# Dilated attention stage: the second head group's projections read the layer input in natural order, and the rewriting of that input between the first two groups goes

## The chip, the cores and the metric

One core of a Trainium2 chip. The metric is the device time of one execution in microseconds (us); lower is better. For the kernel before it is 3289.02 us, the median of 3 runs (3288.62 to 3292.9).

## What is computed

Two layers of an encoder on 1024 tokens of width 1024, all in float32. The change lies in the second layer's token mixer, a dilated sliding-window attention with three groups of 16 heads of width 64. Cut to what matters:

```
DIL_GROUPS = ((128, 1), (512, 4), (2048, 16))
def dilated_mixer(h, pos, w_in, g_q, g_k, rel_bias, w_o):
    proj = (h @ w_in).reshape(B, S, N_DIL_GROUPS, 3, DIL_HEADS, DIL_HEAD_DIM)
    for gi, (window, dilation) in enumerate(DIL_GROUPS):
        q = rms_norm(proj[:, :, gi, 0], g_q[gi])
        k = rms_norm(proj[:, :, gi, 1], g_k[gi])
        o, lse = dilated_group(q, k, proj[:, :, gi, 2], pos, table, window, dilation)
...
def _to_residues(t, dilation):
...
    t = t.reshape((B, L, dilation) + t.shape[2:])
    t = jnp.moveaxis(t, 2, 1)
```

Group 0 has dilation 1, group 1 dilation 4, group 2 dilation 16. Within a group a query sees only tokens whose number has the same remainder by the dilation, so the kernel works on tokens sorted by that remainder ("residue order"). The three outputs are merged by their softmax denominators.

## The kernel before, in words

The kernel runs on one core; a scheduler lays out the instructions of each engine, with the order of TensorE pinned to the program's in this stage. The dilated stage (`dil`) is a list of steps, `steps`: for each group, for each of 8 pairs of heads (`pr`), four steps (`tp`), each of which projects two tiles of 128 tokens. After the 32 steps of groups 0 and 1 stands one `None` step, after those of group 2 six. A `None` step projects nothing: it lets the attention work catch up, which lags the projections by some steps.

One step on TensorE consists of:

- `psav`: the products of the transposed probabilities `pT` with the values, of an earlier step,
- `pss`: 12 score products on `kT`, the stacked queries and keys of an earlier step,
- `psproj`: 24 matmuls for the first tile of 128 tokens,
- `psq`: four transposes of the step before's normalised q and k, `qn`,
- `psproj`: 24 matmuls for the second tile.

The 24 matmuls come from `project` (L1772): 8 chunks of the width, and for each three matmuls of `mm3` (L412 to L416), since each float32 operand is held as a high part and a low part. In them the **layer input is the stationary operand** (128 x 128, so a weight load of 128 tokens by 128 features goes ahead of each matmul), and the weights `wqkh`, `wqkl` are the moving operand of 256 columns.

The input lies transposed in SBUF, features on partitions and tokens along the free axis, in tiles of (128, 2, 512) float32: `hT`, `hTh`, `hTl`, `hsh` and `hsl`, in natural order of tokens. `permute` (L2077) rewrites it. Between groups 0 and 1 it writes 16 new tiles `hTp` in residue order of 4 with 32 copies of 128 x 512, which read every fourth token. Between groups 1 and 2 it writes 16 more `hTp` in residue order of 16 from the first 16, with 64 copies of 128 x 256. The copies go round ACT, DVE, ACT, DVE, POOL (L2092 to L2099). Two of the eight pairs of tiles are rewritten in the last step of a group, six in the `None` step.

From 1668 to 1952 us of the profiled execution group 0 is projected, from 1967 to 2247 us group 1, until 2544 us group 2.

The weights of a pair of heads (`wqkr`, four DMAs of 256 KB) are loaded two steps ahead (`fetch`, L2054, `dil_weights`, L1542 to L1551) by DMAs issued on ACT's queue; ACT and DVE then split them into `wqkh` and `wqkl`. The first pair's load is issued on SP's queue in the stage before. SP's queue also issues the loads of the bias tiles `bt`, the DMA transposes `pT<-ph` and the stores of `U`. All working tiles named here come from one pool of 29 buffers.

Of the kernel before, what the change touches and what calls it, by code (L numbers as in the profile page):

```python
# [9 lines left out]
F32 = mybir.dt.float32  # L10
# [4 lines left out]
AF = mybir.ActivationFunctionType  # L15
ALU = mybir.AluOpType
# [4 lines left out]
P = 128  # L21
# [20 lines left out]
class K:  # L42
# [1706 lines left out]
    def dil(self, at0, at1, tail, wqk, vd):  # L1749


        nc, a, tc = self.nc, self.a, self.tc
# [16 lines left out]
        ln14 = dpool.tile([P, 1], F32, name="ln14", bufs=1)  # L1769
        nc.vector.memset(ln14, 14.0 * math.log(2.0))  # L1770

        def project(h, w, ps, i, t):  # L1772
            tl = slice((t % 4) * P, (t % 4 + 1) * P)
            for d in range(ND):
                self.mm3(ps[:, i * 256 : (i + 1) * 256], h[t // 4](0, d)[:, tl], h[t // 4](1, d)[:, tl],
                         w[d // 4][0][:, d % 4, :], w[d // 4][1][:, d % 4, :], d == 0, d == ND - 1)

        def v_load(g, c):
# [59 lines left out]
        def stacks(u, tp, qn):  # L1838

            ps = PS("psq")  # L1840
            for k in range(2):
                for i in range(2):
                    c = i * 256 + (1 - k) * P
                    nc.tensor.transpose(ps[:, (2 * k + i) * P : (2 * k + i + 1) * P], qn[:, c : c + P], self.ident)
            s1 = 4 + tp % 2
            hi, lo = (u["k"][:, k, :].rearrange("p (s x) -> p s x", x=256)[:, tp : s1 + 1 : s1 - tp, :] for k in range(2))
            x = ps.rearrange("p (k x) -> p k x", k=2)
            nc.scalar.activation(hi, x, AF.Copy)
            nc.vector.tensor_tensor(lo, x, hi.bitcast(F32), op=ALU.subtract)
            for i in range(2):  # L1850
                c = S + (tp % 2 * 2 + i) * P
                u["q"][2 * tp + i] = u["k"][:, :, c : c + P]
# [181 lines left out]
        def um(u, hfs):  # L2034

            u.setdefault("um", [])
            v = Ud[u["pr"]].rearrange("(l t r) k e -> r l t (k e)", t=8, r=2)
            for hf in hfs:
                x = self.G("um", (P, 4, 2, P), F32)
                for i in range(2):  # L2040
                    nc.scalar.dma_start(out=x[64 * i : 64 * i + 64].rearrange("p t k e -> p t (k e)"), in_=v[i][:, 4 * hf : 4 * hf + 4, :])
                u["um"].append(x)
# [2 lines left out]

        steps = []
        for g in range(3):
            steps += [("qk", g, pr, tp) for pr in range(8) for tp in range(4)] + [None] * (1 if g < 2 else 6)
        loads, wts = {}, {}
        mark = len(nc.cur_bb.bb.instructions)  # L2050
        end = max(n for n, x in enumerate(steps) if x is not None)
        firsts = {n: s for n, s in enumerate(steps) if s is not None and s[3] == 0}

        def fetch(n):  # L2054
            if n in firsts:
                loads[n] = self.dil_weights(*firsts[n][1:3], eng=nc.scalar)

        def fetch_split(n):
            if n in firsts:
                wts[firsts[n][0:3]] = loads.pop(n)()  # L2060
# [9 lines left out]
                    vtodo.setdefault(n - 2 + t // 2, []).append(lambda t=t, VS=VS: v_parts(VS["raws"], VS, t))  # L2070
                vtodo.setdefault(n - 2 + t // 2, []).append(lambda VS=VS: VS.pop("raws"))

        h = [at0, at1]
        HT = [at0.tiles, at1.tiles]
        new = None

        def permute(g, dp, k):  # L2077

            for th in range(2):
                x = self.G("hTp", (P, 2, 512))  # L2080
                new[th][k].append(x)
                for oh in range(2):
                    src = HT[oh][k][dp].bitcast(F32)
                    if g == 1:
                        i_ = src.rearrange("p d (l r) -> p d r l", r=4)[:, :, 2 * th : 2 * th + 2, :]
                        copies = [(x.rearrange("p d (r b l) -> p d r b l", r=2, b=2)[:, :, :, oh, :], i_)]
                    else:
                        i_ = src.rearrange("p d (b l a) -> p d a b l", b=2, a=4)
                        o_ = x.rearrange("p d (a b l) -> p d a b l", a=2, b=4)
                        copies = [(o_[:, :, q, 2 * oh : 2 * oh + 2, :], i_[:, :, 2 * th + q]) for q in range(2)]  # L2090
                    for o_, i_ in copies:
                        e = permute.n % 5  # L2092
                        permute.n += 1
                        if e in (0, 2):
                            nc.scalar.activation(o_, i_, AF.Copy)
                        elif e in (1, 3):
                            nc.vector.tensor_copy(o_, i_)
                        else:
                            nc.gpsimd.tensor_scalar(o_, i_, 1.0, 1.0, op0=ALU.mult, op1=ALU.mult)  # L2099

        permute.n = 0
        perms = []
        units = {}
        transposed, scored, ready, carry, stacking, stk, late = [], [], [], [], None, [], []
        src = lambda pp, i, th: oTd[2 * pp : 2 * pp + 2, th, :, i, :].rearrange("r p f -> p r f")
        wts[("qk", 0, 0)] = wqk
        for n in sorted(vtodo):
            if n < 0:
                for f in vtodo.pop(n):
                    f()  # L2110
        for n, step in enumerate(steps):
            fetch(n + 2)
            for f in vtodo.pop(n, ()):
                f()
            if step is None and perms:
                while perms:
                    permute(*perms.pop(0))
                HT = new
                h = [(lambda k, d, t=t: t[k][d // 2][:, d % 2, :]) for t in HT]
            if step is not None and n + 1 < len(steps) and steps[n + 1] is None and step[1] < 2:  # L2120
                new = [[[], []], [[], []]]
                perms = [(step[1] + 1, dp, k) for dp in range(4) for k in range(2)]
                for _ in range(2):
                    permute(*perms.pop(0))
            w = None
            if step is not None:
                kind, g, pr, tp = step
                w = wts[(kind, g, pr)]
                if tp == 0:
                    units[(g, pr)] = {"g": g, "pr": pr, "q": {}, "V": VSs[(g, pr // 2)],  # L2130
                                      "k": D_("kT", (P, 2, S + 512), F32R, 2), "U": self.G("U", (P, 8, P), F32)}
                u = units[(g, pr)]
            fetch_split(n + 1)
            transposed, scored = scored, attend(ready, n > end) if ready else []
            for u_, t_, _ in scored:
                if u_["g"] == 2:
                    if u_["pr"] < 7:
                        if t_ == 7:
                            um(u_, (0, 1))
                    elif t_ in (1, 5):  # L2140
                        um(u_, (t_ // 4,))
            if step is not None:
                ps = PS("psproj")
                project(h, w, ps, 0, 2 * tp)
            ready, carry = carry, []
            stk.append(stacking)
            if len(stk) > 1:
                x = stk.pop(0)
                if x is not None:
                    stacks(*x)  # L2150
                    u_, tp_ = x[:2]
                    if u_["g"] == 2:
                        ready = ready + [(u_, 2 * tp_), (u_, 2 * tp_ + 1)]
                    else:
                        ready = ready + ([(u_, 2 * tp_ - 1), (u_, 2 * tp_)] if tp_ else [(u_, 0)])
                        carry = [(u_, 7)] if tp_ == 3 else []
            if step is not None:
                project(h, w, ps, 1, 2 * tp + 1)
                if step[1:3] == (2, 7):
                    tail(tp)  # L2160
            late, merged[:] = late + merged, []
            while late and (step is None or late[0][1] < n):
                u_, _, ths = late.pop(0)
                emit(u_, ths)
            for x in transposed:
                x[0]["at"] = n
                av(*x)
            stacking = None
            if step is not None:
                stacking = (u, tp, qkstep(u, tp, ps))  # L2170
                if n == end:
                    self.pin_from(mark, mybir.EngineType.PE)
                    banks.close()
                    first = banks.enter_context(tc.tile_pool(name="psY", bufs=4, space=PSUM, reuse_waits="tile"))
                    psp[0] = ctx.enter_context(tc.tile_pool(name="psT", bufs=4, space=PSUM, reuse_waits="tile"))
                    for pp in range(3):
                        self.reload(O, src, pp, 0, nc.sync)
# [171 lines left out]
```

## Time and profile before

| | |
|---|---|
| median of 3 runs | 3289.02 us |
| profiled execution, its own time | 3286.91 us |
| its span in the trace | 3285.1 us |
| mean granted TensorE clock | 0.983 |
| dilated stage's projections, first to last | 1668 to 2544 us |
| loads of `wqkr` issued on ACT's queue, on SP's queue | 92, 4 |

PE stands for TensorE's matmuls, PEld for its weight loads, DVE, ACT and POOL for VectorE, ScalarE and GpSimd, SP for the queue of SyncE. A matmul's recorded duration is longer than the distance between two starts, since they are pipelined: the rate is read from the starts. A row of groups names source line, engine, operation, output and inputs by tile names, shapes and count, then the total in us and the mean in ns, then the idle time of the engine ahead of it with what ended it.

### The profile page before, as it was taken

To read this page: it belongs to the slowest core of one execution; us is meant where nothing else is said; L and a number is where in the kernel's file an instruction comes from. 1 tells how busy PE (TensorE), PEld (TensorE's weight loads), DVE (VectorE), ACT (ScalarE), POOL (GpSimd) and SP (SyncE) were. 2 spreads that over 40 slices of the span, in tenths; PEclk is the share of its full clock that TensorE was granted. 3 is DMA by queue.
4 is the path that set the end of the run, shared out by engine and by line. 5 is a ranking of instruction groups with operands and counts; after the bars stand their busy time and mean duration, and the time that the engine had idled before them with its cause. 6 is when DMAs were issued, how large, how long until landed. Compare 5 with 4: busy or idle time off the path is not lost. (4 is left out here: it accounts for less than half of the span.)

```text
span 3285.1 us, 50852 instructions
## 1 busy us (share of the span) xinstructions
PE 3143.2 (96%) x18034; PEld 2653.5 (81%) x18034; DVE 2406.5 (73%) x4272; ACT 1736.5 (53%) x3507; POOL 878.6 (27%) x1197
## 2 busy tenths in 40 slices
PE   6989999999999999899999989998999899999999
PEld 6877677778888788778889889997988788888887
DVE  5677777757987866787657777777888678778566
ACT  5547787745544433542246676667565355444342
POOL 7455555520111000001133334434333001110010
PEclk8999999999999999999999989998999999999999
DMA  5352233152654788536557877777677635438554
GB/s 189 123 182 91 94 94 100 57 185 87 211 188 162 283 246 281 171 103 210 194 141 167 171 169 171 184 169 160 152 174 180 198 98 203 148 142 321 204 192 129
DMA packets 538990, 552.31 MB, mean 168 GB/s; under 512 B 199493, under 2 KB 421106, under 8 KB 538730
## 3 DMA queue, kind: packets, MB, share of 16 engines
q1 hardware_dynamic: 452362, 418.88, 44.9%
q0 software_dynamic: 27360, 91.31, 7.5%
q10 hardware_dynamic: 59008, 38.81, 4.6%
q8 instruction: 144, 2.36, 0.3%
q14 instruction: 116, 0.95, 0.1%
HBM read 376.17 MB, written 132.62 MB: 155 GB/s over the span
## 5 line engine op out<-in xcount | busy, mean ns | idle before, releaser
L415 PE MATMUL psm<-dl,dh 128*128 128x512 f32 x896 | 351.2, 392 | 8.1 <-DVE dl L122 8.0
L414 PE MATMUL psm<-hf,wf 128*128 128x512 f32 x896 | 350.1, 391 | 2.6 <-ACT wf L121 2.6
L416 PE MATMUL psm<-dh,dl 128*128 128x512 f32 x896 | 350.1, 391 | 0.0
L415 PE MATMUL psm<-hf,wf 128*128 128x512 f32 x896 | 349.2, 390 | 0.0
L416 PE MATMUL psm<-hf,wf 128*128 128x512 f32 x896 | 347.3, 390 | 0.4 <-DVE wf L122 0.4
L414 PE MATMUL psm<-dh,dh 128*128 128x512 f32 x896 | 334.8, 391 | 4.7 <-ACT dh L121 4.7
L414 PE MATMUL psproj<-wqkh,hTp 128*128 128x256 f32 x1024 | 303.2, 296 | 0.0
L415 PE MATMUL psproj<-wqkl,hTp 128*128 128x256 f32 x1024 | 291.1, 284 | 0.0
L416 PE MATMUL psproj<-wqkh,hTp 128*128 128x256 f32 x1024 | 290.9, 284 | 0.0
L121 ACT ACTIVATE dh<-ufr 128x1024 fp32r<-128x1024 f32 x112 | 118.3, 1057 | 174.9 <-PE psm L416 51.4
L415 PEld LDWEIGHTS psm<-dl,dh 128*128 128x128 f32 x896 | 169.0, 189 | 46.0 <-DVE dl L122 11.3
L414 PEld LDWEIGHTS psproj<-wqkh,hTp 128*128 128x128 f32 x1024 | 197.6, 193 | 9.0 <-issue 0.9
L414 PEld LDWEIGHTS psm<-dh,dh 128*128 128x128 f32 x896 | 168.2, 188 | 42.2 <-ACT dh L121 7.0
L414 PEld LDWEIGHTS psm<-hf,wf 128*128 128x128 f32 x896 | 168.6, 188 | 40.3 <-ACT wf L121 5.5
L415 PEld LDWEIGHTS psproj<-wqkl,hTp 128*128 128x128 f32 x1024 | 197.9, 193 | 0.0
L416 PEld LDWEIGHTS psm<-hf,wf 128*128 128x128 f32 x896 | 168.5, 188 | 36.2 <-DVE wf L122 1.1
L416 PEld LDWEIGHTS psm<-dh,dl 128*128 128x128 f32 x896 | 169.1, 189 | 35.1
L416 PEld LDWEIGHTS psproj<-wqkh,hTp 128*128 128x128 f32 x1024 | 197.4, 193 | 0.0
L415 PEld LDWEIGHTS psm<-hf,wf 128*128 128x128 f32 x896 | 168.6, 188 | 34.6
L122 DVE TENSOR_TENSOR dl<-ufr,dh 128x1024 fp32r<-128x1024 f32 x112 | 136.5, 1219 | 78.1 <-ACT dh L121 58.3
L745 DVE TENSOR_REDUCE mx<-pmx 128x1 f32<-128x512 f32 x256 | 165.0, 681 | 27.6 <-PE pmx L743 27.4
L122 POOL TENSOR_TENSOR pl<-p,ph 128x1024 fp32r<-128x1024 f32 x58 | 141.3, 2436 | 136.1 <-ACT ph L121 125.9
(399 smaller groups left out, 8920.9 us busy)
## 6 DMA issues: line engine op xcount, KB each, us to landing
ufr<-uf SPq DMA_DIRECT2D x112, 512.0 KB
adaw<-in_ada_w SPq DMA_DIRECT2D x96, 512.0 KB
w2r<-in_mlp_w SPq DMA_DIRECT2D x96, 512.0 KB
w1r<-in_mlp_w SPq DMA_DIRECT2D x64, 512.0 KB
bt<-bias SPq DMA_DIRECT2D x128, 256.0 KB
wqkr<-in_dil_w_in ACTq DMA_DIRECT2D x92, 256.0 KB
qkv<-st SPq DMA_DIRECT2D x32, 512.0 KB
hraw<-qkv SPq DMA_DIRECT2D x32, 512.0 KB
```

The lines of the kernel that those rows point to most:

```text
L121: nc.scalar.activation(hi, src, AF.Copy)
L122: (lo_eng or nc.vector).tensor_tensor(lo, src, hi.bitcast(F32), op=ALU.subtract)
L414: mm(out, lh, rh, start=first, stop=False)
L415: mm(out, lh, rl, start=False, stop=False)
L416: mm(out, ll, rh, start=False, stop=last)
L745: nc.vector.tensor_reduce(maxes[h][:, 2 * j + b : 2 * j + b + 1], ps, op=ALU.max, axis=AX.X)
```

## The change

`tokens` is new: for group 1 it gives `project` a slice of the natural-order tiles that takes every fourth token, 128 elements 16 bytes apart; for groups 0 and 2 it gives the contiguous slices as before. The `None` step after group 0 goes, and so does the first rewriting. The second rewriting reads the natural-order tiles, every sixteenth token, with 32 copies of 128 x 512 in place of 64 of 128 x 256. The weights of groups 0 and 1 are loaded on SP's queue; those of group 2 stay on ACT's.

```
-        def project(h, w, ps, i, t):
-            tl = slice((t % 4) * P, (t % 4 + 1) * P)
+        def tokens(g, t, k, d):
+            if g == 1:
+                return HT[t % 2][k][d // 2][:, d % 2, :].rearrange("p (l r) -> p r l", r=4)[:, t // 2, :]
+            return HT[t // 4][k][d // 2][:, d % 2, (t % 4) * P : (t % 4 + 1) * P]
+
+        def project(g, w, ps, i, t):
             for d in range(ND):
-                self.mm3(ps[:, i * 256 : (i + 1) * 256], h[t // 4](0, d)[:, tl], h[t // 4](1, d)[:, tl],
+                self.mm3(ps[:, i * 256 : (i + 1) * 256], tokens(g, t, 0, d), tokens(g, t, 1, d),
...
-            steps += [("qk", g, pr, tp) for pr in range(8) for tp in range(4)] + [None] * (1 if g < 2 else 6)
+            steps += [("qk", g, pr, tp) for pr in range(8) for tp in range(4)] + [None] * (0, 1, 6)[g]
...
-                loads[n] = self.dil_weights(*firsts[n][1:3], eng=nc.scalar)
+                loads[n] = self.dil_weights(*firsts[n][1:3], eng=nc.scalar if firsts[n][1] == 2 else nc.sync)
...
-                    src = HT[oh][k][dp].bitcast(F32)
-                    if g == 1:
-                        i_ = src.rearrange("p d (l r) -> p d r l", r=4)[:, :, 2 * th : 2 * th + 2, :]
-                        copies = [(x.rearrange("p d (r b l) -> p d r b l", r=2, b=2)[:, :, :, oh, :], i_)]
-                    else:
-                        i_ = src.rearrange("p d (b l a) -> p d a b l", b=2, a=4)
-                        o_ = x.rearrange("p d (a b l) -> p d a b l", a=2, b=4)
-                        copies = [(o_[:, :, q, 2 * oh : 2 * oh + 2, :], i_[:, :, 2 * th + q]) for q in range(2)]
+                    i_ = HT[oh][k][dp].bitcast(F32).rearrange("p d (l r) -> p d r l", r=16)[:, :, 8 * th : 8 * th + 8, :]
+                    o_ = x.rearrange("p d (r l) -> p d r l", l=64)[:, :, :, 32 * oh : 32 * oh + 32]
```

TensorE at the turn from group 0 to group 1, before: the last score products of group 0's last projected step, and then the `None` step's work, which has no `psproj`.

```order
L1869 MATMUL pss_25191<-kT_24580 128x256
L1869 MATMUL pss_25192<-kT_24580 128x256
L1844 MATMUL psq_25230<-ident,qn_24982 128x128 x4
L1937 LDWEIGHTS pT_25024
L1937 MATMUL psav_25237<-vs_24162,pT_25024 128x192
L1938 LDWEIGHTS pT_25024
```

The same place now: behind the score products stand the first projections of group 1, on `hT` tiles.

```order
L1873 MATMUL pss_25151<-kT_24592 128x256
L1873 MATMUL pss_25152<-kT_24592 128x256
L414 MATMUL psproj_25190<-wqkh_25003,hT_3811_18667 128x256
L415 MATMUL psproj_25190<-wqkl_25004,hT_3811_18667 128x256
L416 MATMUL psproj_25190<-wqkh_25003,hT_3812_18668 128x256
L414 MATMUL psproj_25190<-wqkh_25003,hT_3811_18667 128x256
```

No matmul is added or lost (26351 rows of TensorE in both); the `None` step's attention work moves into the first steps of group 1.

ACT at the same turn, before: between `ph`, the high part of the probabilities, and `wqkh`, the first weights of group 1, stand copies into `hTp`, and the square of the last projection (`dsq`) is in among them.

```order
L1923 ACTIVATE ph_25023<-pd_25039 128x512
L2095 ACTIVATE hTp_25150<-hT_3836_18782 128x4x128
L2095 ACTIVATE hTp_25153<-hT_3837_18783 128x4x128
L2095 ACTIVATE hTp_25156<-hTl_20785 128x4x128
L2095 ACTIVATE hTp_25159<-hsh_19483 128x4x128
L2095 ACTIVATE hTp_25165<-hT_3861_18892 128x4x128
L2095 ACTIVATE hTp_25168<-hT_3861_18892 128x4x128
L1828 ACTIVATE dsq_25126<-psproj_25050 128x512
L2095 ACTIVATE hTp_25171<-hsh_19487 128x4x128
L2095 ACTIVATE hTp_25174<-hsh_19487 128x4x128
L2095 ACTIVATE hTp_25180<-hT_3880_18987 128x4x128
L121 ACTIVATE wqkh_25183<-wqkr_24985 128x1024
```

Now nothing stands between `ph` and the first weights of group 1.

```order
L1927 ACTIVATE ph_24739<-pd_24754 128x512
L121 ACTIVATE wqkh_25003<-wqkr_24855 128x1024
L1832 ACTIVATE dsq_24840<-psproj_24764 128x512
L121 ACTIVATE wqkh_25007<-wqkr_24858 128x1024
L112 ACTIVATE drl_24845<-dms_24841,eps 128x8
```

All 13 copies on ACT are gone there, and the split of the weights follows the attention's rows at once.

SP's queue in group 0 now, at one pair's weight load: it stands behind a DMA transpose and a store of `U`, ahead of the next bias tiles and the next transpose.

```order
L1929 DMA_TRANSPOSE pT_22929<-ph_22928 128x16x128
L1959 DMA U<-U_21796 128x8x128
L1551 DMA wqkr_23181<-in_dil_w_in 128x4x128 x2
L1551 DMA wqkr_23184<-in_dil_w_in 128x4x128 x2
L1882 ISA
L1882 DMA bt_23220<-bias_135 128x2x256
L1882 ISA
L1882 DMA bt_23347<-bias_135 128x2x256
L1929 DMA_TRANSPOSE pT_23066<-ph_23065 128x16x128
```

Before, the four `wqkr` rows of this pair stood on ACT's queue, between `dsq` and the small steps of the normalisation, and here `bt` followed `U` directly.

More of the change, by code (lines that the diff above doesn't have):

```diff
@@ L2071, in dil, with permute @@
                 vtodo.setdefault(n - 2 + t // 2, []).append(lambda VS=VS: VS.pop("raws"))
-        h = [at0, at1]
         HT = [at0.tiles, at1.tiles]
         new = None
-        def permute(g, dp, k):
+        def permute(dp, k):
             for th in range(2):
@@ L2082, in permute @@
                 for oh in range(2):
-                    src = HT[oh][k][dp].bitcast(F32)
-                    if g == 1:
-                        i_ = src.rearrange("p d (l r) -> p d r l", r=4)[:, :, 2 * th : 2 * th + 2, :]
-                        copies = [(x.rearrange("p d (r b l) -> p d r b l", r=2, b=2)[:, :, :, oh, :], i_)]
-                    else:
-                        i_ = src.rearrange("p d (b l a) -> p d a b l", b=2, a=4)
-                        o_ = x.rearrange("p d (a b l) -> p d a b l", a=2, b=4)
-                        copies = [(o_[:, :, q, 2 * oh : 2 * oh + 2, :], i_[:, :, 2 * th + q]) for q in range(2)]
[L2091 to L2097, printed above, removed]
-                        else:
-                            nc.gpsimd.tensor_scalar(o_, i_, 1.0, 1.0, op0=ALU.mult, op1=ALU.mult)
+                    i_ = HT[oh][k][dp].bitcast(F32).rearrange("p d (l r) -> p d r l", r=16)[:, :, 8 * th : 8 * th + 8, :]
+                    o_ = x.rearrange("p d (r l) -> p d r l", l=64)[:, :, :, 32 * oh : 32 * oh + 32]
+                    e = permute.n % 5
+                    permute.n += 1
+                    if e in (0, 2):
+                        nc.scalar.activation(o_, i_, AF.Copy)
+                    elif e in (1, 3):
+                        nc.vector.tensor_copy(o_, i_)
+                    else:
+                        nc.gpsimd.tensor_scalar(o_, i_, 1.0, 1.0, op0=ALU.mult, op1=ALU.mult)
         permute.n = 0
@@ L2118, in dil @@
                 HT = new
-                h = [(lambda k, d, t=t: t[k][d // 2][:, d % 2, :]) for t in HT]
-            if step is not None and n + 1 < len(steps) and steps[n + 1] is None and step[1] < 2:
+            if step is not None and steps[n + 1] is None and step[1] < 2:
                 new = [[[], []], [[], []]]
-                perms = [(step[1] + 1, dp, k) for dp in range(4) for k in range(2)]
+                perms = [(dp, k) for dp in range(4) for k in range(2)]
                 for _ in range(2):
@@ L2143, in dil @@
                 ps = PS("psproj")
-                project(h, w, ps, 0, 2 * tp)
+                project(g, w, ps, 0, 2 * tp)
             ready, carry = carry, []
@@ L2157, in dil @@
             if step is not None:
-                project(h, w, ps, 1, 2 * tp + 1)
+                project(g, w, ps, 1, 2 * tp + 1)
                 if step[1:3] == (2, 7):
```

## The prediction

> **What bounds the kernel now.** I read the page's first lines, then a table by stage, then the matmuls of the stage that changes.
>
> ```profile
> span 3285.1 us, 50852 instructions
> PE 3143.2 (96%) x18034; PEld 2653.5 (81%) x18034; DVE 2406.5 (73%) x4272; ACT 1736.5 (53%) x3507; POOL 878.6 (27%) x1197
> ```
>
> TensorE is busy 96% of the span. The table by stage (group 0, the turn to group 1, group 1 up to its last steps) says where it is not:
>
> ```profile
> core 0: us, PE busy (x) PEld busy (x) DVE busy (x) ACT busy (x) POOL busy (x), PEclk, DMA share, GB/s
> 1668.00:1930.00 262.00, 248.07 (x2262) 237.22 (x2261) 184.16 (x501) 160.42 (x466) 97.33 (x119) 0.98 0.74 162
> 1930.00:1970.00 40.00, 30.06 (x241) 27.36 (x241) 31.61 (x76) 33.57 (x73) 18.55 (x16) 0.80 0.72 163
> 1970.00:2222.00 252.00, 244.44 (x2290) 233.55 (x2290) 183.47 (x517) 161.66 (x481) 104.13 (x156) 1.00 0.78 175
> ```
>
> In group 1 TensorE is idle 252.00 - 244.44 = 7.6 us of 252 at a granted clock of 1.00, while DVE has 27% to spare and ACT 36%. So group 1 lasts as long as its matmuls take, and a nanosecond more per matmul is a nanosecond more of the kernel. At the turn TensorE loses 10 us to idling and has a clock of 0.80 besides.
>
> What one matmul of the projection takes is read from the starts, here two that lie 16 matmuls apart (all 17 are recorded, with no other between):
>
> ```profile
> 2004.04 0.28 PE L415 MATMUL psproj<-wqkl,hTp 128*128 128x256 f32 x1
> ...
> 2005.96 0.28 PE L416 MATMUL psproj<-wqkh,hTp 128*128 128x256 f32 x1
> ```
>
> 1.92 / 16 = 0.120 us each. Ahead of each goes a weight load of 128 x 128. What such a load takes when nothing hides it shows in another place, where 16 loads serve matmuls of a single column:
>
> ```profile
> 1634.36 1.84 PE L237 MATMUL psac<-ones,adacc 128*128 128x1 f32 x16
> 1636.06 0.49 PE L414 MATMUL psv<-wvh,hsh 128*128 128x512 f32 x1
> ```
>
> The next matmul starts 1.70 us later, so a contiguous load takes 1.70 / 16 = 0.106 us. That is the point on which this prediction turns: **the load just fits under the 0.120 us of its matmul, with 0.014 us to spare.** A load that gets slower by more than that shows in full.
>
> **The change part by part.** *1. The strided weight loads.* Group 1 has 8 pairs x 8 tiles x 8 chunks x 3 = 1536 matmuls, and every one now loads 128 columns that lie 16 bytes apart instead of side by side. All weight loads of the kernel before are contiguous, so the trace shows no price; other engines reading at this very stride give the nearest rows, the copies of the first rewriting, with contiguous reads for comparison:
>
> ```profile
> L2095 ACT ACTIVATE hTp<-hT 128x512 fp32r<-128x512 f32 x7 | 7.6, 1129 | 0.0
> L2095 ACT ACTIVATE hTp<-hTp 128x256 fp32r<-128x256 f32 x26 | 15.1, 657 | 0.0
> L121 ACT ACTIVATE wf<-ws 128x512 fp32r<-128x512 f32 x128 | 76.8, 623 | 53.6 <-PE psm L416 21.5 <-DVE ws L1087 15.2 <-DVE us L1087 6.7
> L121 ACT ACTIVATE dh<-ufr 128x1024 fp32r<-128x1024 f32 x112 | 118.3, 1057 | 174.9 <-PE psm L416 51.4 <-PE psm L415 43.5 <-DMA ufr<-uf 30.7
> L2099 POOL TENSOR_SCALAR hTp<-hT 128x512 fp32r<-128x512 f32 x3 | 4.4, 1470 | 0.6 <-DVE hTp L2097 0.6
> L1817 POOL TENSOR_SCALAR vs<-vr 128x512 bf16<-128x512 f32 x48 | 37.1, 775 | 13.0 <-DVE vr L1816 11.5 <-issue 1.6
> L2097 DVE CAST hTp<-hTl 128x512 fp32r<-128x512 f32 x1 | 0.6, 615 | 0.0
> L279 DVE TENSOR_SCALAR xh<-x,xry 128x1024 f32<-128x1024 f32 x16 | 12.0, 756 | 0.6
> ```
>
> ACT with contiguous input: (1057 - 623) / 512 = 0.85 ns an element; at every fourth: (1129 - 657) / 256 = 1.84 ns, 2.2 times as long. POOL: 1470 against 775 ns, 1.9 times. DVE: 615 / 512 = 1.20 ns an element against 756 / 1024 = 0.74, 1.6 times, fixed parts included. A contiguous weight load takes 106 / 128 = 0.83 ns a column, nearly ACT's pace on contiguous data, so ACT's row is the nearest. Twice the load is 0.213 us, ACT's 2.2 times 0.231; a matmul that waits for it adds nothing at the least (as in the 16 loads above) and today's 0.014 us at the most, which gives 0.213 to 0.245 us a matmul. I take 0.22, near twice: 1536 x (0.220 - 0.120) = **+154 us** (ends: +143 and +192 us). The other end is zero: the loads are as quick as now. Below zero nothing, since a strided read has no fewer bytes to fetch. Between lies DVE's pace, 128 x 1.20 = 0.154 us a load.
>
> On what a strided read costs, the Trainium skill speaks with two voices ("SBUF — State Buffer", section "Door 1: The DMA port swizzle"): memory lines have 16 bytes and take two hits each for full speed, and yet four float32 count as a stride for free. Columns 16 bytes apart hit each line once; by the first half the loads pay, by the second they cost nothing and the sum is that of rival A below. The three engines' rows above agree with the first half.
>
> *2. The turn from group 0 to group 1.* The steps there, by the first `psproj` or `pss` of each:
>
> ```profile
> 1932.80 0.39 PE L414 MATMUL psproj<-wqkh,hTh 128*128 128x256 f32 x1
> ...
> 1957.07 0.83 PE L1869 MATMUL pss<-kT 64*128 64x256 f32 x8 [2.93 <-DVE kT L1849]
> ...
> 1965.69 1.23 PE L1869 MATMUL pss<-kT 64*128 64x256 f32 x8 [2.36 <-DVE kT L1849]
> 1966.85 0.58 PE L414 MATMUL psproj<-wqkh,hTp 128*128 128x256 f32 x1
> ...
> 1970.64 0.41 PE L416 MATMUL psproj<-wqkh,hTp 128*128 128x256 f32 x1
> 1970.85 0.41 PE L414 MATMUL psproj<-wqkh,hTp 128*128 128x256 f32 x1
> ```
>
> and a normal step, from one `pss` to the next, takes 8.41 us:
>
> ```profile
> 2219.30 0.98 PE L1869 MATMUL pss<-kT 64*128 64x256 f32 x12
> ...
> 2227.71 0.98 PE L1869 MATMUL pss<-kT 64*128 64x256 f32 x12
> ```
>
> From 1932.80 to 1966.85 are 34.05 us, with two projected steps and the attention work of a third in them: 2 x 8.41 + (8.41 - 48 x 0.120) = 19.5 us of work that stays. The rest, 14.6 us, is waiting for DVE and ACT, which are busy with copies, and a low clock. Behind it the first matmuls of group 1 start 0.21 us apart (last two rows), at half pace: some 19 of them, 19 x 0.09 = 1.7 us. Copies and `None` step gone, this is **-16 us**; at the least half of it (the first strided step might still meet attention work that is late), at the most all.
>
> *3. The second rewriting* has half as many copies of twice the size. ACT: 13 x 1129 = 14.7 us instead of 26 x 657 = 17.1; POOL: 6 x 1470 = 8.8 instead of
>
> ```profile
> L2099 POOL TENSOR_SCALAR hTp<-hTp 128x256 fp32r<-128x256 f32 x13 | 10.6, 829 | 6.0 <-ACT hTp L2095 5.3 <-PE psq L1844 0.6
> ```
>
> No row shows a read 64 bytes apart; I take the price of 16 bytes, so **-2 us**, bounded by -5 and by +5 should it be dearer. TensorE waits for these copies at that turn, so the term is on the path.
>
> *4. Group 1's waits.* Its 7.6 us of idling are
>
> ```profile
> PE psav L1937 <- DMA pT<-ph: 4.6, 5, 1.4
> PE pss L1869 <- DVE kT L1849: 2.3, 4, 0.9
> ```
>
> With 48 x 0.100 = 4.8 us more TensorE time in a step, DVE, ACT and the transposes come in time: **-5 us** (0 to -7).
>
> *5. Weight DMAs on SP's queue.* 60 of them leave ACT (28 for seven pairs of group 0, 32 for group 1):
>
> ```profile
> L1551 ACTq DMA_DIRECT2D wqkr<-in_dil_w_in x92: 374/470/2389, 1663.4 to 2487.9; - x92
> ```
>
> 60 x 0.47 = 28 us of issuing that ACT is rid of, but ACT bounds nothing. On SP the four DMAs of a pair stand ahead of two `bt` loads and a transpose. If they wait for a free buffer or take their 1 MB / 162 GB/s (last column of the table by stage) = 6.5 us on the queue, `pT` comes later, and `psav` waits. The longest such wait in group 0 is 3.1 us:
>
> ```profile
> PE psav L1937 <- DMA pT<-ph: 10.7, 7, 3.1
> ```
>
> Seven pairs x 3.1 = +22 us at the most in group 0; in group 1 the longer steps hide it. ACT's earlier splits could also save a wait or two, -3. I take 0: the loads are two steps (17 us) ahead of their use.
>
> Sum: 154 - 16 - 2 - 5 = +131 us. The profiled execution takes 3286.91 us, 2.1 below the median of the runs; 3289 + 131 = **3420 us**.
>
> **The rivals.** *A, the other side: the strided load stays hidden.* If the loads keep 0.106 us, term 1 is nothing and 16 + 2 us remain as gain: 3271 us, faster. It decides below a load of 0.106 + 0.014 + 18 / 1536 = 0.132 us: there the loads cost what the turns give. For it: the margin of 0.014 us, and that DVE gets on at 1.20 ns an element, so the memory itself is not far off the 0.83 ns wanted. Against: ACT, as quick as the loads on contiguous data, falls to 1.84.
>
> *B, DVE's pace.* A load of 0.154 us, 0.168 us a matmul: 1536 x 0.048 = +74, with the gains of 23 us +51: 3340 us.
>
> *C, the clock falls.* With the array fed only half of the time, TensorE might get the half clock that the first steps after the turn show. A load at half pace is 0.44 us: 1536 x 0.32 - 23 = +468, 3757 us. Against: the turn had waits of 2 to 3 us in a row; strided loads would leave gaps of 0.1 us.
>
> *D, the change gives nothing because SP's queue eats it.* The loads hidden and 18 us lost to late `pT`: 3289 us, no change. For it: the transposes stand behind the loads on one queue. Against: it needs six waits of the longest kind in 15 loads, besides the loads' being hidden.
>
> **How the numbers follow.** Forecast (twice the load): 0.78; its own range 3402 (143 - 30 of gains) to 3475 (192 - 16, and half of the 22 of part 5). A: 0.10, B: 0.06, C: 0.05, D: 0.01. Leaving out A, C, D and the lower half of B's surroundings leaves out about 0.19: the range is 3335 to 3475. A measurement of this kernel tells about 0.2% (6.6 us) from no change: faster 0.10, same 0.02 (D, and loads at the break-even), slower 0.88.
>
> **What would show it.** In group 1's projections the starts of matmuls should lie 0.21 to 0.24 us apart at a granted clock of 1.00, and a step should take about 13 us; group 2's should stay at 0.120. Between the last projection of group 0 and the first of group 1 there should be no wait over 1 us. Waits for `pT` of over 3 us behind a `wqkr` load would show part 5 wrong. Starts 0.12 us apart in group 1 would make the whole prediction wrong, and rival A right.

## The result, and the profile after

The changed kernel takes 3421.19 us (median, 3419.26 to 3425.74) against 3291.43 us for the kernel before in the same runs: 1.0395 times as long, 95% interval 1.0382 to 1.0409. The forecast was 3420 us. The profiled execution took 3420.57 us, its span is 3418.8 us, 133.7 us longer than before.

The page's first lines after: DVE, ACT and POOL are busy for fewer microseconds than before, TensorE for 160 us more.

```profile
span 3418.8 us, 50766 instructions
PE 3303.1 (97%) x18034; PEld 2818.2 (82%) x18034; DVE 2389.3 (70%) x4246; ACT 1724.2 (50%) x3481; POOL 865.0 (25%) x1185
```

The table by stage, for group 0 up to its last two steps and for group 1 with the turn to group 2's first copies:

```profile
core 0: us, PE busy (x) PEld busy (x) DVE busy (x) ACT busy (x) POOL busy (x), PEclk, DMA share, GB/s
1671.00:1927.00 256.00, 246.52 (x2294) 235.62 (x2292) 182.21 (x500) 163.15 (x471) 98.26 (x121) 1.00 0.74 172
1944.80:2389.00 444.20, 443.83 (x2556) 433.97 (x2552) 208.86 (x584) 196.86 (x558) 117.49 (x173) 1.00 0.47 115
```

Group 1 is where the time went: 444 us, TensorE idle for 0.4 us of them, at a granted clock of 1.00, while DVE's share fell from 73% to 47%. Two matmuls of one projection there, 15 starts apart (TensorE's timeline):

```profile
2050.06 0.40 PE L416 MATMUL psproj<-wqkh,hTl 128*128 128x256 f32 x1
...
2053.56 0.40 PE L416 MATMUL psproj<-wqkh,hsl 128*128 128x256 f32 x1
```

3.50 / 15 = 0.2333 us a matmul, where it was 0.120. The turn from group 0 to group 1, last projection of the one, score products, first projection of the other:

```profile
1941.67 0.28 PE L416 MATMUL psproj<-wqkh,hsl 128*128 128x256 f32 x1
...
1943.96 0.98 PE L1873 MATMUL pss<-kT 64*128 64x256 f32 x12
1944.87 0.51 PE L414 MATMUL psproj<-wqkh,hT 128*128 128x256 f32 x1
```

3.2 us stand between the two projections, with `psav` and `pss` in them, where 14.6 us stood before. Of waits, from 1925 to 1975 us, one is left:

```profile
PE psav L1941 <- DMA pT<-ph: 0.8, 1, 0.8
```

The stages against each other, from the starts of their first and last projection matmuls in both timelines (us):

| stretch | before | after | difference |
|---|---|---|---|
| up to the first `psproj` | 1668.84 | 1671.65 | +2.8 |
| first `psproj` to the last but one step of group 0 | 263.96 | 255.37 | -8.6 |
| from there to the first `psproj` of group 1 | 34.05 | 17.85 | -16.2 |
| group 1, first to last `psproj` | 279.95 | 441.81 | +161.9 |
| turn to group 2 | 19.23 | 18.53 | -0.7 |
| group 2 | 278.05 | 275.23 | -2.8 |
| rest of the span | 741.0 | 738.4 | -2.7 |

The first and the last row are no effect of the change: over all the traces of this document the first `psproj` stands anywhere from 1668.0 to 1673.5 us, and the rest of the span takes 735 to 743 us.

### The profile page after: what moved, and what is told of

It is laid out like the page before. It is cut to its first block, busy times and chain, and to the rows that moved or that the text cites. A ratio compares the mean times of both kernels' runs of the same rounds, so it can differ in the third digit from the quotient of the medians.

```text
span 3418.8 us, 50766 instructions
## 1 busy us (share of the span) xinstructions
PE 3303.1 (97%) x18034; PEld 2818.2 (82%) x18034; DVE 2389.3 (70%) x4246; ACT 1724.2 (50%) x3481; POOL 865.0 (25%) x1185
## 5 line engine op out<-in xcount | busy, mean ns | idle before, releaser
L1943 DVE TENSOR_REDUCE U<-psav 128x128 f32<-128x384 f32 x192 | 103.3, 551 | 163.9 <-PE psav L1942 163.8
L415 PEld LDWEIGHTS psm<-dl,dh 128*128 128x128 f32 x896 | 169.5, 189 | 46.7 <-DVE dl L122 11.3
L1928 POOL TENSOR_TENSOR ph<-pd,ph 128x512 f16<-128x512 f32 (+1 forms) x121 | 121.4, 1009 | 245.8 <-ACT ph L1927 185.2
L414 PE MATMUL psproj<-wqkh,hT 128*128 128x256 f32 x512 | 180.1, 352 | 0.0
L1839 POOL TENSOR_TENSOR qn<-qn,dgain 128x256 f32<-128x256 f32 x96 | 83.2, 867 | 378.3 <-DVE qn L1837 336.2
L416 PE MATMUL psproj<-wqkh,hT 128*128 128x256 f32 x512 | 174.0, 340 | 0.0
L415 PE MATMUL psproj<-wqkl,hT 128*128 128x256 f32 x512 | 173.5, 339 | 0.0
```

What stands on the lines that cost most here:

```text
L414: mm(out, lh, rh, start=first, stop=False)
L415: mm(out, lh, rl, start=False, stop=False)
L416: mm(out, ll, rh, start=False, stop=last)
L1839: nc.gpsimd.tensor_tensor(qq, qq, gain[:, g : g + 1, :].unsqueeze(1).broadcast_to([P, 2, 2, 64]), op=ALU.mult)
L1928: (nc.gpsimd if i or g == 2 else nc.vector).tensor_tensor(lo, p, hi, op=ALU.subtract)
L1943: nc.vector.tensor_reduce(u["U"][:, t, :].rearrange("p (e d) -> p e d", e=2), ps[:, 0:384].rearrange("p (e k d) -> p e d k", e=2, k=3), op ...
```

## The experiments

**Theory**: a weight load pays for each 16-byte line of memory that its columns touch; at stride four that is 128 lines a load, the load becomes longer than its matmul and alone sets the pace of group 1; the rest of the change is a gain. **Rivals**: the longer steps come from the other edits (order, weights on SP's queue); any stride but one costs the same; load and matmul no longer run beside each other.

### The change without the stride (e1_contig)

```
-                return HT[t % 2][k][d // 2][:, d % 2, :].rearrange("p (l r) -> p r l", r=4)[:, t // 2, :]
+                return HT[t % 2][k][d // 2][:, d % 2, t // 2 * P : t // 2 * P + P]
```

> The changed kernel, but group 1's projections load contiguous slices of the natural-order tiles (wrong tokens for group 1, so its output is not the reference's; instructions, copies and queues stay as they are). Theory (the stride alone makes the loads long, and everything else of the change is a gain): starts 0.120 us apart in group 1, 3421 - 1536 x 0.113 = 3247 us, plus up to 10 us where the waits that the longer steps hid come back: 3247 to 3257 us, faster than before by over 1%. Rival (the stretch comes from something else of the change, such as the order on TensorE or the weights on SP's queue): starts stay well above 0.120 us and the time stays above 3300 us.

Measured: 3258.08 us against 3287.32, ratio 0.9911 (0.9896 to 0.9927). Two matmuls of one projection in group 1, 8 starts apart, so 0.96 / 8 = 0.120 us each:

```profile
2054.04 0.28 PE L414 MATMUL psproj<-wqkh,hsh 128*128 128x256 f32 x1
...
2055.00 0.28 PE L416 MATMUL psproj<-wqkh,hsl 128*128 128x256 f32 x1
```

With everything of the change but the stride the kernel is 29 us faster than before; that is 0.9%, where over 1% was expected, and 1 us above the expected 3247 to 3257 us. The stride alone costs 3421 - 3258 = 163 us, or 130 + 29 = 159 us if each kernel is taken against the one before in its own runs. That is less than 1536 x 0.113 = 174 us, for with short steps the waits come back: in group 1 TensorE idles 8.0 us of 277.6, where it idled for nothing under the strided loads.

### Other strides (e2_stride2, e6_stride3, e3_stride8)

```
+                return HT[t % 2][k][d // 2][:, d % 2, t // 4 : t // 4 + 255 : 2]
...
+                return HT[t % 2][k][d // 2][:, d % 2, t // 4 : t // 4 + 382 : 3]
...
+                return HT[t % 2][k][d // 2].rearrange("p d f -> p (d f)")[:, t // 2 : t // 2 + 1017 : 8]
```

> The changed kernel, but group 1's projections load every second token (wrong tokens for group 1). Theory (a load pays for each 16-byte line that it touches, 0.233 us for 128 lines, so 1.82 ns a line): 64 lines, 0.117 us, which hides nearly under the matmul: starts 0.12 to 0.13 us apart, 3247 to 3270 us. Rival (any stride but one halves the rate): starts 0.233 us apart, 3421 us.

> The changed kernel, but group 1's projections load every third token, 12 bytes apart (wrong tokens for group 1): of four columns two share a line and two stand alone, 96 lines a load. Theory (1.82 ns a line): 0.175 us, about 3421 - 1536 x 0.058 = 3332 us. Rival (all or nothing: full pace as long as a stride is below 16 bytes): starts 0.12 us apart, 3264 us as with every second token.

> The changed kernel, but group 1's projections load every eighth element of a tile (wrong tokens for group 1), 32 bytes apart. Theory (price by lines touched): 128 lines as at stride four, starts 0.233 us apart, 3421 us. Rival (price by the distance between columns, or by bytes spanned): longer than 0.233 us, up to 0.47 us and 3421 + 1536 x 0.233 = 3779 us at twice the span.

Measured, one execution each: 3263.76 us at stride two, 3327.21 at three, 3427.14 at eight. The starts in TensorE's timeline, at stride two 17 apart, at three 12 apart, at eight 17 apart:

```profile
2053.11 0.28 PE L415 MATMUL psproj<-wqkl,hTh 128*128 128x256 f32 x1
...
2055.15 0.29 PE L414 MATMUL psproj<-wqkh,hsh 128*128 128x256 f32 x1
```

```profile
2054.47 0.34 PE L415 MATMUL psproj<-wqkl,hTh 128*128 128x256 f32 x1
...
2056.55 0.34 PE L415 MATMUL psproj<-wqkl,hsh 128*128 128x256 f32 x1
```

```profile
2055.78 0.40 PE L416 MATMUL psproj<-wqkh,hT 128*128 128x256 f32 x1
...
2059.88 0.41 PE L415 MATMUL psproj<-wqkl,hT 128*128 128x256 f32 x1
```

| columns apart | lines a load | us a matmul | ns a line |
|---|---|---|---|
| 4 bytes (e1_contig) | 32 | 0.120, load hidden | |
| 8 bytes | 64 | 0.120, load hidden | at most 1.88 |
| 12 bytes | 96 | 0.1733 | 1.81 |
| 16 bytes (the change) | 128 | 0.2333 | 1.82 |
| 32 bytes | 128 | 0.2412 | 1.88 |

The loads' own records, from 1975 to 2180 us, say the same (count, then shortest, median and longest ns; contiguous, then 8, 12, 16 and 32 bytes apart). They overlap as the matmuls' do, so they are longer than the distance between starts:

```profile
L415 PEld LDWEIGHTS psproj<-wqkl,hT x184: 187/192/193, 1980.3 to 2171.9; 128*128 128x128 f32 x184
L415 PEld LDWEIGHTS psproj<-wqkl,hT x184: 194/195/199, 1980.8 to 2173.5; 128*128 128x128 f32 x184
L415 PEld LDWEIGHTS psproj<-wqkl,hT x147: 261/261/266, 1975.2 to 2174.6; 128*128 128x128 f32 x147
L415 PEld LDWEIGHTS psproj<-wqkl,hT x117: 329/329/330, 1974.9 to 2172.1; 128*128 128x128 f32 x117
L415 PEld LDWEIGHTS psproj<-wqkl,hT x113: 337/338/345, 1974.8 to 2174.5; 128*128 128x128 f32 x113
```

The price goes by lines, about 1.8 ns each, as soon as that exceeds the 0.83 ns a column of a contiguous load. Stride three lies where the theory put it (0.175 us, 3332 us), not at either end; both all-or-nothing rivals fall. From 16 to 32 bytes only 3% are added, so it isn't distance that costs. The two halves of what the Trainium skill says ("SBUF — State Buffer", section "Door 1: The DMA port swizzle") part here: that a 16-byte line needs two hits for full speed agrees with these rows (195 ns recorded with two hits a line, 192 contiguous, 329 with one), that a stride of four float32 is free does not, for a weight load. With two hits a line the load stays within the 0.120 us of its matmul; whether by itself it takes the 0.106 us of a contiguous one or 64 x 1.82 ns = 0.117 us, these runs don't tell.

### Does the load run beside its matmul? (e5_halves, e10_wide)

```
+            for c in ((slice(0, 128), slice(128, 256)) if g == 1 else (slice(0, 256),)):
...
+                    self.mm3(ps[:, i * 256 : (i + 1) * 256][:, c], tokens(g, t, 0, d), tokens(g, t, 1, d),
+                             w[d // 4][0][:, d % 4, c], w[d // 4][1][:, d % 4, c], d == 0, d == ND - 1)
```

> The changed kernel, but in group 1 each matmul of 256 columns is made as two of 128, each with a strided load of its own (3072 instead of 1536; the output is complete). Theory (the load alone sets the pace, the matmul runs beside it): starts stay 0.233 us apart, 3421 + 1536 x 0.233 = 3779 us. Rival (load and matmul stand one behind the other, 0.107 us of 256 columns and 0.126 us of a load that is hardly longer than before): starts 0.18 us apart, 3421 + 3072 x 0.18 - 1536 x 0.233 = 3616 us.

Measured, in one execution: 3831.62 us. TensorE's starts in group 1, 13 apart in matmuls of half the size, then the stretch of 400 us in the table by stage, then one step's 12 score products:

```profile
2099.82 0.44 PE L415 MATMUL psproj<-wqkl,hTh 128*128 128x128 f32 x1
...
2102.85 0.44 PE L416 MATMUL psproj<-wqkh,hsl 128*128 128x128 f32 x1
```

```profile
1950.00:2350.00 400.00, 400.00 (x1901) 392.50 (x1901) 93.91 (x258) 87.55 (x247) 51.66 (x78) 0.54 0.25 61
```

```profile
2051.93 1.65 PE L1874 MATMUL pss<-kT 64*128 64x256 f32 x12
```

3.03 / 13 = 0.233 us, the pace of the 256-column matmuls: the load alone sets it. The 52 us above the 3779 expected are not in these starts but in the other matmuls of a step: the 12 score products take 1.65 us, 0.98 in the change, and all that stands between two steps' projections takes 4.04 us instead of 2.35, between a step's two halves 0.96 instead of 0.59. That is 2.1 us a step, 66 us in 32 steps; the turn to group 2, 7.6 us shorter than in the change, gives some back. The granted clock in this stage is 0.54 (it is 1.00 in the change's); that it is the clock which stretches them is argued, not tried.

The other way round, twice the columns under each strided load (the second half is the neighbouring chunk's weights):

```
+                if g == 1:
+                    wh, wl = (x.rearrange("p d f -> p (d f)")[:, d % 4 // 2 * 512 : d % 4 // 2 * 512 + 512] for x in w[d // 4])
+                    self.mm3(ps, tokens(g, t, 0, d), tokens(g, t, 1, d), wh, wl, d == 0, d == ND - 1)
+                    continue
```

> The changed kernel, but in group 1 each matmul takes 512 columns of weights instead of 256 (the neighbouring chunk's besides, and the second tile of tokens overwrites the first, so its output is not the reference's): twice the work under the same 1536 strided loads. Theory (the strided load alone sets the pace and hides any matmul that is shorter): a contiguous 512-column matmul stands at 0.227 us in this kernel's MLP, so starts stay 0.233 us apart, 3421 us. Rival (a strided load and its matmul get in each other's way, reading the same memory): starts above 0.25 us apart, over 3447 us.

Measured, in one execution: 3431.53 us, 10 us more than the change. Starts 17 apart, and below them 512-column matmuls of the MLP with contiguous loads, six apart, in the kernel before:

```profile
2049.06 0.40 PE L416 MATMUL psproj<-wqkh,hTl 128*128 128x512 f32 x1
...
2053.08 0.40 PE L415 MATMUL psproj<-wqkl,hsh 128*128 128x512 f32 x1
```

```profile
2740.07 0.39 PE L414 MATMUL psm<-hf,wf 128*128 128x512 f32 x1
...
2741.43 0.39 PE L414 MATMUL psm<-hf,wf 128*128 128x512 f32 x1
```

4.02 / 17 = 0.2365 us for double the work, 3 ns above the load's own pace; 1.36 / 6 = 0.227 us with contiguous loads. Load and matmul hardly hinder each other: under a matmul of 512 columns a strided load costs 0.010 us, under one of 256 it costs 0.113.

### The weights' queue by itself (e4_sp_weights)

```
-                loads[n] = self.dil_weights(*firsts[n][1:3], eng=nc.scalar)
+                loads[n] = self.dil_weights(*firsts[n][1:3], eng=nc.scalar if firsts[n][1] == 2 else nc.sync)
```

> The kernel before with one edit: the weights of groups 0 and 1 are loaded on SP's queue. In the trace of the changed kernel group 0's projections up to the third last step took 8.6 us less than before, though nothing of the projections differs there. Theory (ACT rid of the DMA issues is in time more often): group 0 gains 8 us, group 1 about as much, 3273 to 3283 us. Rival (the gain comes from elsewhere, the order that the scheduler chose or the missing turn): 3291 us, no change; or the transposes queue behind the loads and it is slower by some us.

Measured: 3282.74 us against 3287.32, ratio 0.9985 (0.9976 to 0.9994), a gain of about 5 us. Group 0's start, its last but one step and the start of group 1:

```profile
1673.49 0.28 PE L414 MATMUL psproj<-wqkh,hT 128*128 128x256 f32 x1
...
1927.91 0.39 PE L414 MATMUL psproj<-wqkh,hTh 128*128 128x256 f32 x1
...
1967.67 0.58 PE L414 MATMUL psproj<-wqkh,hTp 128*128 128x256 f32 x1
```

From its first projection to its last but one step group 0 takes 254.4 us (before 263.96, after the change 255.37): the edit, with the order that the scheduler then lays out, explains the whole gain of group 0. All twelve traces with these loads on SP's queue have 253.3 to 256.8 us there; of the kernel before there is one trace. Group 1 gains 2 us (277.9 against 279.95), not the 8 expected. In group 0, waits for the transposes come to

```profile
PE psav L1937 <- DMA pT<-ph: 5.9, 5, 1.7
```

against 10.7 us in the kernel before: the loads in front of the transposes on SP's queue did not hold these up. The granted clock there is 1.00, before 0.98.

The turn takes 39.8 us instead of 34.05 and eats more than half of the gain again. There TensorE's waits for transposes, from 1928 to 1970 us, and what SP's queue issues ahead of the second transpose are:

```profile
PE psav L1937 <- DMA pT<-ph: 12.9, 2, 11.3
1943.35 15.70 SPq L1878 DMA_DIRECT2D bt<-bias  x4
```

The longest wait is 11.3 us, before it was 3.3. Four `bt` loads take the queue 15.7 us, and the transpose comes behind them; no `wqkr` load stands among them. Whether the moved loads brought this about is not shown. In the change, which has no `None` step, the turn has no such wait.

### Neither all strided nor all rewritten (e7_gradual2, e8_gradual1, e9_gradual_first, e11_evenodd)

These keep the gains and spread the rewriting over the first steps of group 1, so that strided loads last for a few steps only:

```
+            for dp, k in made:
+                HT[2][k].add(dp)
...
+                perms = [(step[1] + 1, dp, k) for k in range(2) for dp in range(4)]
+            for _ in range(min(2, len(perms))):
+                x = perms.pop(0)
+                permute(*x)
+                made.append(x[1:])
```

`tokens` takes a part from the new tiles if it stands in `HT[2]`, and at stride four from the old ones if not.

> Neither all strided nor all rewritten: no None step after group 0, weights of groups 0 and 1 on SP's queue, and the rewriting is spread over steps, two of its eight parts in each from the last step of the old group on, high parts first; a projection loads what has been rewritten contiguously and the rest at stride four. The second rewriting does the same and keeps its None step. Theory: strided loads remain for 8/12 + 4/12 + 2/12 of a step, 14/12 x 48 x 0.113 = 6 us, on top of the 3258 us of the contiguous run: 3264 us, faster than before by 0.7%, and the second turn may give some more. Rival (the copies hold up DVE and ACT in the steps into which they are moved, as in the kernel before): 3280 to 3291 us.

> As the kernel with two parts a step, but one part a step. Theory (strided loads cost 0.113 us each): 10 + 8 + 6 + 4 + 3 + 2 + 1 = 34 twelfths of a step, 34/12 x 48 x 0.113 = 15 us at each turn (at the second less, the None step takes one part): 3258 + 15 + 10 = 3283 us, slower than with two parts. Rival (what costs is the copies' crowding, not the loads): faster than with two parts, 3258 to 3264 us.

Measured: two parts a step 3273.77 us against 3291.20, ratio 0.9950 (0.9933 to 0.9966); one part a step 3282.21 us, ratio 0.9982 (0.9968 to 0.9996). The order of the two is the theory's: more strided loads, more time. Against the 3264 us hoped for, 10 us are lost; in the first turn TensorE waits

```profile
PE psav L1943 <- DMA pT<-ph: 4.2, 2, 2.4
```

where the contiguous run waits 3.0 us, and the second turn became longer: from the last but one projection of group 1 to the fifth of group 2's, 48.6 us instead of 43.4 (45.8 in the contiguous run). The forecast also left out the 24 strided loads that the second rewriting leaves, an estimated 24 x 0.113 = 2.7 us. Where all of the 10 us went is open.

The second turn put back into one go:

```
-            for _ in range(min(2, len(perms))):
+            for _ in range(min(len(perms) if step is None else 2, len(perms))):
```

> The kernel with two parts of the rewriting a step at the first turn, but at the second turn as before: two parts in the last step of group 1, six in the None step. With the gradual second turn TensorE took 48.6 us from the last but one projection of group 1 to the fifth of group 2's, in the kernel before 43.4. Theory (the second turn was better in one go, since there the None step is there anyway): 5 us less than 3274, 3269 us, 0.7% faster than before. Rival (the second turn's length is set by late attention work, not by where the copies stand): 3274 us.

Measured: 3275.30 us against 3290.84, ratio 0.9954 (0.9941 to 0.9967): no difference from the gradual second turn, the rival holds as far as this can tell.

Since stride two is free, the first rewriting need only sort each tile into even and odd tokens:

```
+                        copies = [(x.rearrange("p d (q m) -> p d q m", q=2), src.rearrange("p d (m q) -> p d q m", q=2))]
...
+            return y.rearrange("p (q l s) -> p q s l", q=2, s=2)[:, t // 2 % 2, t // 4, :]
```

> The gradual kernel with the second turn in one go, but the first rewriting only sorts the tokens of each tile into even and odd ones, 16 copies of 128 x 1024 that read every second element; group 1 loads from that every second element, 8 bytes apart, and at stride four what is not rewritten yet. Theory (a price for each 16-byte line touched, for ACT as for the loads): stride-two loads stay hidden at 0.120 us, as in the run with every second token, and ACT's copies take 1.06 us for 1024 elements where they took 1.13 for 512; with half the copying at the first turn some 4 us less than the 3275 us of the gradual kernel, 3271 us. Rival (copies at the turn are hidden as they are): 3275 us, the same. Were stride-two loads from this layout not free: up to 1536 x 0.113 = 174 us more.

Measured: 3271.53 us against 3286.08, ratio 0.9964 (0.9951 to 0.9977), so no faster than the others by these intervals. Where it acts it does what was expected: from the last but one step of group 0 to group 1 its timeline has 16.8 us (e7 20.7, e9 18.8, the kernel before 34.05), and the copies that read every second element, listed as count, then shortest, median and longest ns, cost for 1024 elements what they cost at stride four for 512 (ACT and DVE: 1129 and 615 ns before; two other DVE copies took 686 and 1657 ns):

```profile
L2103 ACT ACTIVATE hTp<-hT x4: 1129/1148/1155, 1919.9 to 1960.6; 128x1024 fp32r<-128x1024 f32 x4
L2105 DVE CAST hTp<-hTh x2: 686/690/694, 1919.2 to 1921.5; 128x1024 fp32r<-128x1024 f32 x2
```

Its second turn has one wait of 12 us, and still, by the same two projections, is the shortest of these versions at 43.2 us (e7 48.6, e9 46.6):

```profile
PE psav L1947 <- DMA pT<-ph: 13.8, 2, 12.0
```

All four versions are faster than both kernels, e8 by 0.2%, the other three by 0.4 to 0.5%; which of these three is best stays open.

## Why the prediction was right, point by point

**1. The strided loads, forecast +154 us.** Right in mechanism: the load became longer than its matmul, and each of 1536 matmuls waits for it. The size was 20 us short: 1536 x (0.2333 - 0.120) = +174 us. A step takes 13.9 us, where about 13 were named as a sign. The prediction had the ratio in hand, ACT's 2.2 times; 0.106 x 2.2 = 0.233 is what was measured, within the ends given. Choosing "near twice" instead of the nearest row's own ratio was the mis-sized choice. That ACT's ratio hits so well is one match: POOL's 1.9 and DVE's 1.6 would have missed.

**2. The turn, forecast -16 us.** Of these 14.6 us were for the stretch from group 0's last but one step to group 1, where -16.2 us were measured. The other 1.7 us, the half-pace start of group 1, fall into group 1's row. Strided loads cover them, but in e1_contig the first 24 matmuls start within 2.86 us, where it was 4.77: 1.9 us gone.

**3. The second rewriting, forecast -2 us.** Measured -0.7, but that can't be put down to the copies: in the kernels with the very same second rewriting this turn takes from 10.9 us (e5) to 22.1 us (e1_contig). On ACT and POOL reads 64 bytes apart cost what reads 16 bytes apart cost, as assumed (median 1094 ns on ACT, 1449 on POOL; before 1129 and 1470 as means). DVE's shortest copy stayed at 0.6 us too, but the median of its copies from `hT` rose from 633 to 1474 ns, for a reason that was not looked into:

```profile
L2091 ACT ACTIVATE hTp<-hT x7: 1074/1094/1117, 2359.8 to 2388.7; 128x512 fp32r<-128x512 f32 x7
...
L2095 POOL TENSOR_SCALAR hTp<-hT x3: 1117/1449/1453, 2356.1 to 2386.8; 128x512 fp32r<-128x512 f32 x3
```

At that turn TensorE's longest wait is for one late transpose. Ahead of it on SP's queue stands a store of `U`, and DVE turned to `U` only behind its last copy (until 2392.9 us), so the copies may have a part in it:

```profile
PE psav L1941 <- DMA pT<-ph: 10.4, 1, 10.4
```

**4. Group 1's waits, forecast -5 us.** Measured: 161.9 - 174.0 = -12 us. Some 2 of them belong to the half-pace start (item 2). Of the rest, 7.6 us are the whole idling in the prediction's table, of which it took 5, and 1.9 us (24.80 - 22.85) lie in the last steps of the group, behind the table's end at 2222 us, where copies had already begun:

```profile
2222.00:2246.80 24.80, 22.85 (x199) 21.84 (x198) 20.32 (x51) 20.67 (x59) 12.15 (x18) 0.93 0.89 187
```

**5. The queue, forecast 0.** Measured -8.6 us in group 0, and e4 shows that it is the queue's edit. The step that failed is "ACT bounds nothing". For the whole kernel e4 gains 5 us only. The sign named for this part, a wait for `pT` of over 3 us behind a `wqkr` load, did not come in group 0: the longest wait there is 1.8 us. The edit takes about 28 us of issuing off ACT and shortens waits for `pT`; which of ACT's instructions were held up wasn't tried.

So the total came out within 2 us because the loads were set 20 us too low and the gains of items 2 to 5 nearly 15 us too low (37.6 us instead of 23); another 3 us fell in stretches for which nothing was forecast. The right total is partly luck; the sign and the size of the large term are not: e1 and e6 put the price on the stride itself.

The rivals: A (loads stay hidden) is refuted by 0.2333 us, though its world exists (e1, e2) and is even better than 3271 us. B (DVE's pace) is refuted. C (the clock falls) did not happen with 256 columns, but it does with 128 (e5, 0.54), and there the strided loads keep their 0.233 us, where C had 0.44. D fails on both counts: the loads are not hidden, and the queue gained time.

## What to carry to other kernels

In these runs a weight load was free only while it was shorter than its matmul: with 256 moving columns there was a margin of 14 ns, and one access pattern made each matmul wait 113 ns, eight times as much. Where an operand must be read with a stride, count the 16-byte lines it touches and compare 1.8 ns a line with the matmul's 0.120 us (256 columns) or 0.227 (512): stride two in float32 was free here, stride four was not, and a matmul of 512 columns hid all but 0.010 us of it. Only float32 was tried. Price such an access by the nearest measured row, with that row's own ratio; here it was another engine's whose pace on contiguous data was the same.

## What the runs showed of the hardware that was not expected

The time of a strided load did not change with the granted clock: 0.233 us at 1.00 (the change) and at 0.54 (e5). The clock itself fell where the matmuls took a smaller part of the time. An estimated 0.107 us of streaming in each 0.233 us kept 1.00 (0.227 us for 512 columns less 0.120 for 256 gives 0.107 for 256). Half of that in the same 0.233 us, without a single wait of TensorE in the records, gave 0.54, in the one execution of e5. Where between the two the clock falls, and whether nothing else in e5 has a part in it, was not tried.
